# HGRN2 in a two-layer streaming encoder: all products inside the chunks of a group issued in one step, the levels prepared one group ahead

## The chip, the cores and the metric

The kernel runs on one core of a Trainium2 chip. The metric is the device time of one execution in microseconds; of the kernel before there are three runs.

## What is computed

Each of two layers is `x <- x + W_out . concat[mLSTM | retention | SSD | HGRN2](RMSNorm(x) W_in)` for 1024 tokens of a new stream and 8 running streams of 16 tokens. The change lies in HGRN2, a recurrence with a forget decay of each channel, computed here in chunks:

```python
def hgrn_block(s_prev, xs):
    q, k, v, lf = xs
    b = jnp.cumsum(lf, axis=2)
    diff = b[:, :, :, None, :] - b[:, :, None, :, :]
    w = jnp.exp(jnp.where(causal_tril(l)[:, :, None], diff, -jnp.inf))
    s = jnp.einsum("bhtk,bhsk,bhtsk->bhts", q, k, w)
    o = jnp.einsum("bhts,bhsv->bhtv", s, v) + jnp.einsum("bhtk,bhkv->bhtv", q * jnp.exp(b), s_prev)
    s_new = jnp.exp(bl)[..., None] * s_prev + jnp.einsum("bhsk,bhsv->bhkv", k * jnp.exp(bl[:, :, None, :] - b), v)
```

The decay is a vector over the channels, so the scores `s` of a chunk aren't one product of queries and keys: each block of the lower triangle needs queries and keys that refer to a token between them.

## The kernel before

The residual stream is feature-major and lies in SBUF in nine chunks of 128 tokens (eight of the prompt, one with the 8 x 16 sample tokens), in three groups of three chunks. Weight slabs of 256 columns stream once per layer. Weights and activations are split into two parts (hi and lo), and three matmuls per k tile add hi x hi, lo x hi and hi x lo: lines 422 to 424 for products with tokens on the partitions, 401 to 403 with features there. A projection k step below is such a triple.

The mixers are units: four of HGRN2 (h0 to h3, one per head), and pairs of heads of mLSTM (m), retention (r) and SSD (s). The order in a layer is h0, r0, s0, m0, h1, r1, s1, m1, h2, h3, then the two halves of the output projection. The mixer of a unit is a generator (`mix`) and runs beside the projection of the next unit: h0 beside r0, h1 beside r1, h2 beside h3, h3 beside the output projection. `merge` interleaves them: it takes a mixer step whenever the share of steps done falls behind the share of projection steps done, times a pace (0.9 for h beside h, whose last 6 steps go on into the next unit; 1 for h beside r). So the number `steps` of a unit sets how far apart its steps lie. `self.after(1, f)` puts f off by one mixer step, `self.later` by projection steps. There is one queue per engine, in the order in which the program issues; TensorE does what stands there in order, so a matmul that waits holds up the projection behind it.

In HGRN2 `ev_qf` (lines 1413 to 1443) makes queries, keys and running sums of decays from the projection's results, and `fours` (1445) refers the decays to the middle of four tokens, with two products on GpSimd. In `mix`, for each group:

- `base` (1536) multiplies keys and queries inside blocks of 32 tokens, 12 matmuls of 32 columns (line 1544), of which the triangles of four tokens are wanted; it also clears two tiles on GpSimd (1546, 1547), and a copy under a mask takes the result one step later (1548).
- `level` (1524) prepares one of five levels, with blocks of 64, 32, 16, 8 and 4 tokens (li = 0 to 4): two subtractions on VectorE, an exponential on ScalarE, and one step later a product with the keys on GpSimd and one with the queries on VectorE (all products and differences go through the helper at line 210).
- `pick` (1553) multiplies one level, 12 matmuls of 16 columns for levels 2 to 4 (line 1562), 3 of 64 x 64 or 6 of 32 x 32 for levels 0 and 1 (1574), and copies the result one step later. `diag` puts the blocks of 32 into the scores' tile ST.
- `prep` decays queries and keys for the state, `keys` transposes the keys (1594), `state` (1613) and `state_s` (1634) update the states, `out` (1652, 1654) forms the outputs, `post` norms and scales them (1672), `fin` transposes them back (1681).

The main loop takes six steps per group: base, then levels 0 to 4, with `level` three levels ahead, and the output of the group before beside them. At the start the first two levels are prepared over five steps (in h0 and h1; three in h2 and h3):

```python
for li in range(-1, NLEV):
    if li < 0:
        base(g, W)
        prep(g, W)
    else:
        pick(g, W, li)
    if li + LOOK < NLEV:
        level(W, g, li + LOOK)
```

Of the kernel before, what the change touches and what calls it, by code (L numbers as in the profile page):

```python
# [26 lines left out]
D = 1024  # L27
# [16 lines left out]
# the order of the mixers (their projections; a mixer works beside the next one's projection), and the  # L44
# feature tiles of the mixed sequence that each half of the output projection takes
# [73 lines left out]
class Kernel:  # L119
# [24 lines left out]
    # ---- tiles  # L144
# [25 lines left out]
    # ---- work put off by a number of projection steps, so that the tensor engine doesn't wait for it  # L170
# [13 lines left out]
    # ---- the same by a number of mixer steps: what waits for another engine is issued when that is done  # L184
# [11 lines left out]
    # ---- small helpers  # L196
# [21 lines left out]
    # ---- setup  # L218
# [24 lines left out]
    def vectors(self):  # L243
        """Per-channel vectors, brought to channel-on-partition form by one transpose each."""
# [61 lines left out]
    # ---- weight slabs  # L306
# [129 lines left out]
    # ---- residual, norms  # L436
# [4 lines left out]
    def fetch_x(self, g):  # L441
        """Token-major input halves [chunk][half] of group g."""
# [93 lines left out]
    # ---- gates  # L536
# [8 lines left out]
    # ---- per-layer gate preparation  # L545
    def gate_prep(self, l, gt):
# [9 lines left out]
        # SSD: softplus, decays  # L556
# [4 lines left out]
        self.sg = sg  # dt, b, exp(b), exp(total - b), exp(total), exp(total) of the sample streams  # L561
# [47 lines left out]
        # mLSTM: input gates, stabilisers  # L609
# [91 lines left out]
    def streams_in(self, po, zq, state, first):  # L701
        """Adds what the states before the streams give to the sample chunk, in column tiles of two streams."""
# [4 lines left out]
    def km(self, src, which):  # L707
        """For each stream src [128 tokens, 128] with the other streams' rows set to zero."""
# [11 lines left out]
    # ---- mLSTM  # L720
# [247 lines left out]
    # ---- retention  # L968
# [167 lines left out]
    # ---- SSD  # L1136
# [270 lines left out]
    # ---- HGRN2  # L1407
    def unit_h(self, l, h):
# [76 lines left out]
        def mix():  # L1485
# [29 lines left out]
            def prep(g, W):  # L1515
                # decayed queries and keys for the state
# [19 lines left out]
            def base(g, W):  # L1536
                """Groups of four tokens; like the levels inside 32 tokens, in column tiles of 32 tokens, the result by
                token of the tile."""
                sc = self.ps("sc")
                for c in range(3):  # L1540
                    for j in range(4):
                        rs = slice(32 * j, 32 * j + 32)
                        ts = slice(128 * c + 32 * j, 128 * c + 32 * j + 32)
                        nc.tensor.matmul(sc[rs, 32 * c:32 * c + 32], k[g][:, ts], q[g][:, ts], start=True, stop=True)
# [3 lines left out]
                self.after(1, lambda: nc.vector.copy_predicated(D, self.lev[:, LEVW - 96:], sc[:, 0:96]))  # L1548

            def pick(g, W, li):  # L1550
                hs = 64 >> li
# [459 lines left out]
```

## Time and profile before

| | us |
|---|---|
| runs, median of 3 | 2415.31 |
| runs, lowest and highest | 2415.06, 2416.91 |
| span of the profiled execution | 2412.0 |
| TensorE busy in it | 2341.9 (97%) |
| VectorE busy | 1382.3 (57%) |
| ScalarE busy | 1078.9 (45%) |
| GpSimd busy | 933.7 (39%) |
| mean granted clock of TensorE | 0.993 |

The profile gives one execution. Its span runs from the first to the last instruction; the time of a run is taken around it. Matmuls are pipelined: their records overlap, and what one costs is read from start to start. A matmul of fp32 operands leaves two records, so 12 matmuls of the fours are 24 in the timeline. A busy share is an average over stages with different limits, so it doesn't tell what a change in one stage is worth.

### The profile page before, as it was taken

The numbers are of one execution on the slowest core, as the hardware profiler recorded it, in microseconds if no ns is written. First come the engines' busy times: TensorE is split into PE (matmuls) and PEld (weight loads), VectorE is DVE, ScalarE is ACT, GpSimd is POOL, SyncE is SP. The second block draws the span as 40 slices with busy tenths as digits, with TensorE's granted clock in tenths as the row PEclk, the third lists the DMA queues.
The fourth block names the chain that finished last, engine by engine and source line by source line (L and its number), as shares of the span: only waits on it lengthen the run. The fifth ranks groups of instructions, "written<-read, shape, count | busy, mean of one in ns | idle before, by whom it ended". The sixth has DMA issues, their size and how long they took to land.

```text
span 2412.0 us, 50123 instructions
## 1 busy us (share of the span) xinstructions
PE 2341.9 (97%) x19264; PEld 2239.2 (93%) x19264; DVE 1382.3 (57%) x3491; ACT 1078.9 (45%) x2780; POOL 933.7 (39%) x1107
## 2 busy tenths in 40 slices
PE   7999999999999999999989999999999999899998
PEld 7899999999999988899988999999899999889998
DVE  4756753673765366544367376536737654666443
ACT  6344573434555345433244445634344653454332
POOL 2442344253334235423136333432633452345353
PEclk9999999999999999999999999999999999999999
DMA  5112233221123222536411212322111333125552
GB/s 151 37 49 57 71 89 77 67 59 52 49 83 95 71 62 74 158 116 212 133 37 38 61 54 83 86 69 72 48 50 53 100 75 82 49 84 168 161 168 82
DMA packets 273738, 204.09 MB, mean 85 GB/s; under 512 B 57908, under 2 KB 264140, under 8 KB 273500
## 3 DMA queue, kind: packets, MB, share of 16 engines
q1 hardware_dynamic: 273180, 200.81, 29.1%
q8 instruction: 152, 2.49, 0.5%
q14 instruction: 86, 0.70, 0.1%
q0 software_dynamic: 320, 0.09, 0.0%
HBM read 148.53 MB, written 52.29 MB: 83 GB/s over the span
## 4 chain that ended last, share of the span: by engine, by line
PE 86%; DVE 7%; ACT 3%; issue 2%; DMA 1%; POOL 1%; SPq 0%; DVEq 0%; ACTq 0%; POOLq 0%
PE w L422 12%; PE w L401 12%; PE w L424 11%; PE w L423 11%; PE w L402 11%; PE w L403 11%; DVE f L210 3%; ACT f L213 2%; PE w L1299 1%; PE w L1652 1%; PE w L1562 1%; PE w L1613 1%; DVE c L210 1%; PE w L486 1%; PE w L1052 1%
## 5 line engine op out<-in xcount | busy, mean ns | idle before, releaser
L422 PE MATMUL w<-hi,hnh 128*128 128x256 f32 (+1 forms) x2592 | 767.4, 296 | 0.0
L424 PE MATMUL w<-hi,hnl 128*128 128x256 f32 (+1 forms) x2592 | 730.7, 282 | 1.6 <-DVE hnl L489 1.4
L423 PE MATMUL w<-lo,hnh 128*128 128x256 f32 (+1 forms) x2592 | 729.8, 282 | 0.0
L422 PEld LDWEIGHTS w<-hi,hnh 128*128 128x128 f32 x2592 | 492.7, 190 | 11.4 <-issue 7.7
L424 PEld LDWEIGHTS w<-hi,hnl 128*128 128x128 f32 x2592 | 490.9, 189 | 2.2 <-DVE hnl L489 2.0
L423 PEld LDWEIGHTS w<-lo,hnh 128*128 128x128 f32 x2592 | 491.6, 190 | 1.2
L213 ACT ACTIVATE f<-f 128x384 f32<-128x384 f32 (+1 forms) x475 | 244.1, 516 | 435.1 <-DVE f L210 271.9
L213 ACT ACTIVATE c<-c 128x512 f32<-128x512 f32 (+3 forms) x398 | 211.8, 534 | 286.3 <-DVE c L543 205.4
L210 POOL TENSOR_TENSOR f<-f,f 128x384 f32<-128x384 f32 (+2 forms) x268 | 226.6, 853 | 286.3 <-ACT f L213 211.8
L401 PE MATMUL w<-hnh,hi 128*128 128x384 f32 x960 | 336.1, 350 | 0.0
L210 POOL TENSOR_TENSOR lo<-raw,hi 128x512 fp32r<-128x512 f32 x148 | 195.3, 1320 | 346.1 <-ACT hi L200 293.6
L403 PE MATMUL w<-hnh,lo 128*128 128x384 f32 x960 | 324.8, 338 | 0.0
L402 PE MATMUL w<-hnl,hi 128*128 128x384 f32 x960 | 324.3, 338 | 0.0
L401 PE MATMUL w<-mxh,hi 128*128 128x384 f32 x768 | 267.4, 348 | 0.0
L403 PE MATMUL w<-mxh,lo 128*128 128x384 f32 x768 | 259.7, 338 | 0.0
L402 PE MATMUL w<-mxl,hi 128*128 128x384 f32 x768 | 259.5, 338 | 0.0
L210 POOL TENSOR_TENSOR c<-c,c 128x512 f32<-128x512 f32 (+2 forms) x120 | 129.7, 1089 | 229.5 <-ACT c L213 187.0
L210 DVE TENSOR_TENSOR lo<-raw,hi 128x512 fp32r<-128x512 f32 x140 | 112.8, 806 | 135.8 <-ACT hi L200 135.6
L401 PEld LDWEIGHTS w<-hnh,hi 128*128 128x128 f32 x960 | 181.7, 189 | 6.8 <-issue 5.9
L402 PEld LDWEIGHTS w<-hnl,hi 128*128 128x128 f32 x960 | 181.6, 189 | 0.0
L403 PEld LDWEIGHTS w<-hnh,lo 128*128 128x128 f32 x960 | 181.1, 189 | 0.0
L210 DVE TENSOR_TENSOR c<-c,w 128x384 f32<-128x384 f32 (+1 forms) x124 | 73.4, 595 | 184.9 <-PE w L403 116.9
(302 smaller groups left out, 3892.8 us busy)
## 6 DMA issues: line engine op xcount, KB each, us to landing
raw<-in_w_in SPq DMA_DIRECT2D x224, 128.0 KB
raw<-in_w_in SPq DMA_DIRECT2D x112, 256.0 KB
c<-mixd SPq DMA_DIRECT2D x96, 192.0 KB
raw<-in_w_out SPq DMA_DIRECT2D x64, 256.0 KB
xd<-c SPq DMA_DIRECT2D x66, 192.0 KB
mixd<-c SPq DMA_DIRECT2D x48, 256.0 KB
c<-xd SPq DMA_DIRECT2D x60, 192.0 KB
c<-sscr SPq DMA_DIRECT2D x36, 256.0 KB
```

Of the source, the lines that this page charges most:

```text
L210: (self.nc.vector if e == "v" else self.nc.gpsimd).tensor_tensor(out=out, in0=a, in1=b, op=op)
L213: self.nc.scalar.activation(out=out, in_=in_, func=func, scale=scale, bias=bias, **k)
L401: nc.tensor.matmul(o, hi[:, k, ms], xhi[:, k, :], start=(k == 0), stop=False)
L402: nc.tensor.matmul(o, hi[:, k, ms], xlo[:, k, :], start=False, stop=False)
L403: nc.tensor.matmul(o, lo[:, k, ms], xhi[:, k, :], start=False, stop=(k == KT - 1))
L422: nc.tensor.matmul(o, xhi[:, k, ts], hi[:, k, :w], start=(k == 0), stop=False)
L423: nc.tensor.matmul(o, xhi[:, k, ts], lo[:, k, :w], start=False, stop=False)
L424: nc.tensor.matmul(o, xlo[:, k, ts], hi[:, k, :w], start=False, stop=(k == KT - 1))
L486: nc.tensor.matmul(ps[:, cs], tiles[cc][k // 4][:, 128 * (k % 4):128 * (k % 4) + 128], dg[:, cs], start=True, stop=True)
L1052: nc.tensor.matmul(po[h], w[:, h], v[j][:, i, h], start=(c in (0, 8)), stop=(c == 0 or (c < 8 and h == 1)))
L1299: nc.tensor.matmul(po[:, 64 * h:64 * h + 64], pt[:, h], x_[:, 64 * h:64 * h + 64], start=True, stop=True)
L1562: nc.tensor.matmul(sc[rs, 16 * c:16 * c + 16].rearrange("p (n t) -> p n t", t=hs), xt, half(xt), start=True, stop=True)
```

## The change

The instructions are the same on every engine, apart from their order. `base` and `pick` become `fresh` (the two clears) and `gram`, which issues the products of the fours and all five levels at once into two PSUM tiles; one step later a single function makes all the copies out of them. A group takes five steps instead of six: `gram` with the first output chunk of the group before; `keys` with the other two; `post`; `state`; `fin`. The levels of the next group are prepared in its first three steps, two, two and one, with `prep` beside the last and `fresh` a step later. For the first group these are four steps ahead of the first `gram`, without the empty steps of before. `steps` is 29 for all units (it was 31 for h0 and h1). Shortened:

```diff
-            def base(g, W):
-                sc = self.ps("sc")
...
-                self.after(1, lambda: nc.vector.copy_predicated(D, self.lev[:, LEVW - 96:], sc[:, 0:96]))
-            def pick(g, W, li):
...
+            def fresh(W):
+                W["ST"], W["D"] = ST, D = self.f(), self.t(96)
+                nc.gpsimd.memset(ST, 0.0)
+                nc.gpsimd.memset(D, 0.0)
+            def gram(g, W):
+                sc, sb = self.ps("sc"), self.ps("sc")
+                half = lambda a, hs: a.rearrange("p (n e t) -> p n e t", e=2, t=hs)[:, :, 1]
+                mm = lambda o, a, b_: nc.tensor.matmul(o, a, b_, start=True, stop=True)
+                at = lambda li: 96 + 48 * (li - 2)
+                for c in range(3):
+                    for j in range(4):
+                        ts = slice(128 * c + 32 * j, 128 * c + 32 * j + 32)
+                        mm(sc[32 * j:32 * j + 32, 32 * c:32 * c + 32], k[g][:, ts], q[g][:, ts])
+                for li in range(2, NLEV):
...
+                            mm(o.rearrange("p (n t) -> p n t", t=hs), xt, half(xt, hs))
+                for li in (1, 0):
...
+                            mm(sb[64 * j:64 * j + hs, 192 * li + hs * c:192 * li + hs * c + hs], xt[:, 0:hs], xt[:, hs:2 * hs])
+                def evac():
...
+                    diag(W)
+                self.after(1, evac)
...
-            for _ in range(2 if h < 2 else 0):
-                yield
             level(Ws[0], 0, 0)
-            yield
             level(Ws[0], 0, 1)
-            for _ in range(2 if h < 2 else 2):
-                yield
+            yield
+            level(Ws[0], 0, 2)
+            level(Ws[0], 0, 3)
+            yield
+            level(Ws[0], 0, 4)
+            fresh(Ws[0])
+            yield
+            prep(0, Ws[0])
+            yield
             for g in range(NG):
                 W = Ws[g]
...
+                V = Ws[g - 1] if g > 0 else None
+                for s in range(5):
+                    if s == 0:
+                        gram(g, W)
+                        if V:
+                            out(g - 1, V, 0)
+                    elif s == 1:
                         keys(g, W)
...
+                    if g + 1 < NG:
+                        for li in ((0, 1), (2, 3), (4,), (), ())[s]:
+                            level(Ws[g + 1], g + 1, li)
+                        if s == 2:
+                            prep(g + 1, Ws[g + 1])
+                        if s == 3:
+                            fresh(Ws[g + 1])
                     yield
...
-        return dict(runs=[("tm", ev_vg), ("fm", ev_qf)], mix=mix, steps=31 if h < 2 else 29, ...
+        return dict(runs=[("tm", ev_vg), ("fm", ev_qf)], mix=mix, steps=29, ...
```

Where instructions went is seen in three places. On TensorE, at the first group of h1 beside r1, the fours (line 1544) stood alone between projection matmuls, before:

```order
L423 MATMUL w_6227<-lo_5728,hnh_231 128x256
L424 MATMUL w_6227<-hi_5727,hnl_232 128x256
L1544 MATMUL w_6237<-f_5725,f_5787 32x32 x12
L422 MATMUL w_6227<-hi_5727,hnh_231 128x256
L423 MATMUL w_6227<-lo_5728,hnh_231 128x256
L424 MATMUL w_6227<-hi_5727,hnl_232 128x256
```

and now (line 1547 is the one matmul call of `gram`):

```order
L424 MATMUL w_6162<-hi_5703,hnl_232 128x256
L1547 MATMUL w_6219<-f_5701,f_5763 32x32 x12
L1547 MATMUL w_6219<-f_6104 32x16 x12
L1547 MATMUL w_6219<-f_6108 32x16 x12
L1547 MATMUL w_6219<-f_6143 32x16 x12
L1547 MATMUL w_6220<-f_6075 32x32 x6
L1547 MATMUL w_6220<-f_6071 64x64 x3
L422 MATMUL w_6162<-hi_5703,hnh_231 128x256
```

All six products stand together, five k steps of the projection ahead of where the fours stood (923 k steps into the kernel, now 918; in h2 beside h3 1671 and now 1675).

On GpSimd at the same place, from the last decayed queries and keys (two products of 128x384) on; c are tiles of r1's rotary embedding, lo is the weight split. Before:

```order
L210 TENSOR_TENSOR f722_6039<-f722_6039,f729_6082 128x384
L210 TENSOR_TENSOR f726_6068<-f726_6068,f730_6083 128x384
L210 TENSOR_TENSOR lo15_6129<-raw15_0_5731,hi15_6128 128x2x256
L210 TENSOR_TENSOR c735_6154<-c733_6150,c734_6151 128x8x32
L210 TENSOR_TENSOR c735_6154<-c734_6151,c733_6150 128x8x32
L210 TENSOR_TENSOR c735_6154<-c735_6154,cst_107 128x512
L210 TENSOR_TENSOR f732_6140<-f732_6140,f685_5787 128x3x64
L210 TENSOR_TENSOR f737_6176<-f737_6176,f685_5787 128x6x32
```

and now:

```order
L210 TENSOR_TENSOR f708_6015<-f708_6015,f715_6058 128x384
L210 TENSOR_TENSOR f712_6044<-f712_6044,f716_6059 128x384
L210 TENSOR_TENSOR f718_6071<-f718_6071,f671_5763 128x3x64
L210 TENSOR_TENSOR f719_6075<-f719_6075,f671_5763 128x6x32
L210 TENSOR_TENSOR lo15_6125<-raw15_0_5707,hi15_6124 128x2x256
L210 TENSOR_TENSOR f720_6104<-f720_6104,f671_5763 128x12x16
L210 TENSOR_TENSOR f721_6108<-f721_6108,f671_5763 128x24x8
L1538 MEMSET f723_6147 128x384
L1539 MEMSET t724_6148 128x96
L210 TENSOR_TENSOR c727_6158<-c725_6154,c726_6155 128x8x32
L210 TENSOR_TENSOR c727_6158<-c726_6155,c725_6154 128x8x32
L210 TENSOR_TENSOR c727_6158<-c727_6158,cst_107 128x512
```

The next row is level 4, `f722_6143`. Levels 0 to 3 and the clears now stand ahead of the rotary products, and level 4 right behind them.

On VectorE in h2 beside h3, around the scaling of the second group's output (line 1672). Before:

```order
L543 TENSOR_SCALAR f_11839<-w_11786 128x384
L1425 SCALAR_TENSOR_TENSOR f_11841<-f_11841,oml,f_11840 128x384
L1427 TENSOR_SCALAR f_11839<-f_11839 128x384
L1434 SCALAR_TENSOR_TENSOR f_11839<-ones,f_11839 128x128 x3
L210 TENSOR_TENSOR lo_11760<-raw_1_11241,hi_11759 128x2x256
L210 TENSOR_TENSOR t_11859<-f_11839 128x96
L1453 SCALAR_TENSOR_TENSOR f_11860<-t_11859,f_11839 128x384
L1458 TENSOR_SCALAR f_11839<-t_11859 128x384
L1566 COPY_PREDICATED t_11692<-lev,w_11814 128x2x16
L1672 SCALAR_TENSOR_TENSOR f_11824<-w_11742,s_11823,c_10333 128x128
L1672 SCALAR_TENSOR_TENSOR f_11824<-w_11742,s_11823,c_10462 128x128 x2
```

and now (the line is 1678):

```order
L1678 SCALAR_TENSOR_TENSOR f_11749<-w_11678,s_11748,c_10285 128x128
L1678 SCALAR_TENSOR_TENSOR f_11749<-w_11678,s_11748,c_10414 128x128 x2
L1629 SCALAR_TENSOR_TENSOR f_11781<-f_11571,bl_11038,w_11778 128x128
L1629 SCALAR_TENSOR_TENSOR f_11781<-f_11781,bl_11038,w_11778 128x128
L543 TENSOR_SCALAR f_11815<-w_11782 128x384
L1425 SCALAR_TENSOR_TENSOR f_11817<-f_11817,oml,f_11816 128x384
L1427 TENSOR_SCALAR f_11815<-f_11815 128x384
L1434 SCALAR_TENSOR_TENSOR f_11815<-ones,f_11815 128x128 x3
```

The scaling now stands ahead of the gate chain of h3's projection (lines 543 to 1458) instead of behind it.

## Rows read from the trace of the kernel before

**Rows 1.** The page's head and totals: busy us, share of the span, instructions, by engine.

```profile
span 2412.0 us, 50123 instructions
...
PE 2341.9 (97%) x19264; PEld 2239.2 (93%) x19264; DVE 1382.3 (57%) x3491; ACT 1078.9 (45%) x2780; POOL 933.7 (39%) x1107
```

**Rows 2.** Waits of TensorE by line and releaser: us in total, times, longest.

```profile
PE w L1594 <- DVE f L210: 12.2, 8, 2.9
...
PE w L1681 <- DVE f L1672: 8.1, 3, 3.1
...
PE w L1574 <- POOL f L210: 6.9, 4, 3.2
PE w L1562 <- POOL f L210: 4.6, 6, 1.2
PE w L1613 <- ACT f L200: 4.4, 7, 0.7
```

**Rows 3.** TensorE's timeline, h1 beside r1: start us, us, line, operation, records.

```profile
502.94 0.28 PE L424 MATMUL w<-hi,hnl 128*128 128x256 f32 x1
503.14 0.40 PE L1544 MATMUL w<-f,f 128*32 128x32 f32 x24
503.47 0.39 PE L422 MATMUL w<-hi,hnh 128*128 128x256 f32 x1
...
505.93 0.28 PE L424 MATMUL w<-hi,hnl 128*128 128x256 f32 x1
506.14 0.56 PE L1574 MATMUL w<-f 128*64 128x64 f32 x6
506.63 0.38 PE L422 MATMUL w<-hi,hnh 128*128 128x256 f32 x1
506.85 0.28 PE L423 MATMUL w<-lo,hnh 128*128 128x256 f32 x1
```

**Rows 4.** TensorE's timeline, level 3 and the state product, second group.

```profile
538.21 0.38 PE L1562 MATMUL w<-f 128*32 128x16 f32 x24
538.52 0.94 PE L1613 MATMUL w<-c,f 128*128 128x128 f32 x6
```

**Rows 5.** GpSimd's timeline, h1 beside r1, in brackets the idle time before.

```profile
497.22 2.14 POOL L210 TENSOR_TENSOR f<-f,f 128x384 f32<-128x384 f32 x2 [1.73 <-ACT f L213]
499.32 1.41 POOL L210 TENSOR_TENSOR lo<-raw,hi 128x512 fp32r<-128x512 f32 x1
500.69 1.54 POOL L210 TENSOR_TENSOR c<-c,c 128x256 f32<-128x256 f32 x2
502.31 1.40 POOL L210 TENSOR_TENSOR c<-c,cst 128x512 f32<-128x512 f32 x1
503.67 1.27 POOL L210 TENSOR_TENSOR f<-f,f 128x192 f32<-128x192 f32 x2
...
508.05 0.41 POOL L1546 MEMSET f<- 128x384 f32 x1
```

**Rows 6.** VectorE's timeline, h1 beside r1.

```profile
496.41 0.62 DVE L210 TENSOR_TENSOR f<-f 128x192 f32<-128x192 f32 x2
...
498.41 2.53 DVE L210 TENSOR_TENSOR f<-f 128x192 f32<-128x192 f32 x2
```

**Rows 7.** VectorE and TensorE where h0 beside r0 starts; TensorE where h2 beside h3 does.

```profile
97.45 0.59 DVE L210 TENSOR_TENSOR f<-f 128x192 f32<-128x192 f32 x2
...
99.68 0.40 PE L1544 MATMUL w<-f,f 128*32 128x32 f32 x24
...
896.70 0.40 PE L1544 MATMUL w<-f,f 128*32 128x32 f32 x24
```

**Rows 8.** Stretches: their length, busy us of five engines, granted clock, DMA share, GB/s.

```profile
907.40:910.80 3.40, 3.17 (x37) 2.84 (x37) 2.57 (x5) 0.79 (x2) 3.07 (x4) 0.50 0.04 13
...
917.40:934.70 17.30, 15.88 (x221) 14.48 (x220) 13.42 (x37) 8.81 (x27) 7.19 (x11) 1.00 0.21 63
523.50:544.90 21.40, 21.40 (x272) 20.37 (x272) 17.51 (x48) 10.16 (x28) 13.22 (x21) 1.00 0.26 73
```

More of the change, by code (lines that the diff above doesn't have):

```diff
@@ L1558, in pick @@
                     for c in range(n):
                         for j in range(4):
-                            rs = slice(32 * j, 32 * j + 32)
                             xt = x[:, 128 * c + 32 * j:128 * c + 32 * j + 32]
-                            nc.tensor.matmul(sc[rs, 16 * c:16 * c + 16].rearrange("p (n t) -> p n t", t=hs), xt, half(xt),
-                                             start=True, stop=True)
-                    cp = lambda a: a.rearrange("p (n t) -> p n t", t=hs)
-                    mk = self.lev[:, 48 * (li - 2):48 * (li - 2) + 16 * n]
@@ L1566, in pick @@
-                    self.after(1, lambda: nc.vector.copy_predicated(half(D[:, 0:32 * n]), cp(mk), cp(sc[:, 0:16 * n])))
-                    if li == NLEV - 1:
-                        self.after(1, lambda: diag(W))
-                    return
-                for c in range(n):
-                    for j in range(64 // hs):
-                        rs = slice(64 * j, 64 * j + hs)
-                        xt = x[:, 128 * c + 64 * j:128 * c + 64 * j + 2 * hs]
-                        nc.tensor.matmul(sc[rs, hs * c:hs * c + hs], xt[:, 0:hs], xt[:, hs:2 * hs], start=True, stop=True)
@@ L1576, in put @@
-                def put():
-                    for j in range(64 // hs):
-                        rs = slice(64 * j, 64 * j + hs)
-                        self.copy(sv(W["ST"][rs], n)[:, :, 64 * j + hs:64 * j + 2 * hs],
-                                  sc[rs, 0:hs * n].rearrange("p (c t) -> p c t", t=hs), BIG[li])
-                self.after(1, put)
+                            o = sc[32 * j:32 * j + 32, at(li) + 16 * c:at(li) + 16 * c + 16]
+                            mm(o.rearrange("p (n t) -> p n t", t=hs), xt, half(xt, hs))
@@ new lines, in gram @@
+                for li in (1, 0):
+                    hs = 64 >> li
+                    x, w = W["X"].pop(li)
+                    widths[li] = n = w // 128
+                    for c in range(n):
+                        for j in range(64 // hs):
+                            xt = x[:, 128 * c + 64 * j:128 * c + 64 * j + 2 * hs]
+                            mm(sb[64 * j:64 * j + hs, 192 * li + hs * c:192 * li + hs * c + hs], xt[:, 0:hs], xt[:, hs:2 * hs])
+                def evac():
+                    D = W["D"]
+                    nc.vector.copy_predicated(D, self.lev[:, LEVW - 96:], sc[:, 0:96])
+                    for li in range(2, NLEV):
+                        hs, n = 64 >> li, widths[li]
+                        cp = lambda a: a.rearrange("p (n t) -> p n t", t=hs)
+                        mk = self.lev[:, 48 * (li - 2):48 * (li - 2) + 16 * n]
+                        nc.vector.copy_predicated(half(D[:, 0:32 * n], hs), cp(mk), cp(sc[:, at(li):at(li) + 16 * n]))
+                    for li in (0, 1):
+                        hs, n = 64 >> li, widths[li]
+                        for j in range(64 // hs):
+                            rs = slice(64 * j, 64 * j + hs)
+                            self.copy(sv(W["ST"][rs], n)[:, :, 64 * j + hs:64 * j + 2 * hs],
+                                      sb[rs, 192 * li:192 * li + hs * n].rearrange("p (c t) -> p c t", t=hs), BIG[li])
+                    diag(W)
@@ L1691, in mix @@
             SS = {}
-            for _ in range(2 if h < 2 else 0):
-                yield
             level(Ws[0], 0, 0)
+            level(Ws[0], 0, 1)
             yield
-            level(Ws[0], 0, 1)
-            for _ in range(2 if h < 2 else 2):
-                yield
+            level(Ws[0], 0, 2)
[6 more added lines that the diff above has]
+            yield
             for g in range(NG):
                 W = Ws[g]
-                for li in range(-1, NLEV):
-                    if li < 0:
-                        base(g, W)
-                        prep(g, W)
-                    else:
-                        pick(g, W, li)
-                    if li + LOOK < NLEV:
-                        level(W, g, li + LOOK)
-                    elif g + 1 < NG:
-                        level(Ws[g + 1], g + 1, li + LOOK - NLEV)
-                    if li == 1:
-                        keys(g, W)
-                    if li == 3:
+                V = Ws[g - 1] if g > 0 else None
[5 more added lines that the diff above has]
+                    elif s == 1:
+                        keys(g, W)
+                        if V:
+                            out(g - 1, V, 1)
+                            out(g - 1, V, 2)
+                    elif s == 2 and V:
+                        post(g - 1, V)
+                    elif s == 3:
                         state(g, W)
@@ L1716, in mix @@
                             load_states()
-                    if g > 0:
-                        V = Ws[g - 1]
-                        for cc in {0: (0,), 1: (1, 2)}.get(li, ()):
-                            out(g - 1, V, cc)
-                        if li == 2:
-                            post(g - 1, V)
-                        if li == 4:
-                            fin(g - 1, V)
-                            Ws[g - 1] = None
+                    elif s == 4 and V:
+                        fin(g - 1, V)
+                        Ws[g - 1] = None
+                    if g + 1 < NG:
[5 more added lines that the diff above has]
+                            fresh(Ws[g + 1])
                     yield
@@ L1742, in mix @@
             yield
-        return dict(runs=[("tm", ev_vg), ("fm", ev_qf)], mix=mix, steps=31 if h < 2 else 29, gate=(lambda: self.gate_prep(l, gt)) if h == 0 else None)
+        return dict(runs=[("tm", ev_vg), ("fm", ev_qf)], mix=mix, steps=29, gate=(lambda: self.gate_prep(l, gt)) if h == 0 else None)
     def mix_load(self, l, half, g):
```

16 lines of the change are left out of this document (4 added, 12 removed).

## The prediction

> **What bounds the kernel now.** I read the totals of the page first, then the waits of TensorE, then the timelines of the places where the change acts. TensorE is busy 97% of a span of 2412.0 us [rows 1]; VectorE (57%) and GpSimd (39%) have room on average. So time can only come from what TensorE does between the projection's matmuls, from its waits, or from its clock. The waits at HGRN2's lines sum to 12.2 + 8.1 + 6.9 + 4.6 + 4.4 = 36.2 us [rows 2]; they sit at the first group of a unit and in the stretch of h2 beside h3. The runs' median is 2415.3 us, 3.3 above the profiled span; I take what lies around the span as unchanged, make the sum on the span and add it to the median. A difference under 0.2% (4.8 us) can't be told from none.
>
> **Part 1, fewer bursts on TensorE.** A burst of small products inside the projection costs more than its own matmuls. For level 0 alone the last projection matmul starts at 505.93 and the second one after the burst at 506.85: 0.92 us where two ordinary pitches take 0.235 (0.117 each), a price of 0.68 [rows 3]. For the fours the step back begins 0.53 after the last projection matmul; with the same slow first pitch behind it (0.22) and less 0.235 that is 0.51. Level 2 stands alone like the fours: 0.50. Level 3 has the state product behind it: 0.31 from its start to that product, 0.21 to get in as with the fours, less the 0.12 that would pass without it: 0.40 [rows 4]; levels 1 and 4 (ahead of the key transposes and of the last transposes) cost 0.40 each by the same pattern. A group pays 0.51 + 0.68 + 0.50 + 3 x 0.40 = 2.9 us. The one burst that replaces them issues the same matmuls. Inside the fours' burst 503.47 - 503.14 = 0.33, less one pitch to get out, for 24 records: 0.0087 each. So 96 records of fours and levels 2 to 4 take 0.83; level 1 about 0.18 and level 0 about 0.36 (0.49 less 0.13); getting in 0.08, out 0.13, the slow first pitch 0.10: 1.7 us. That is **1.2 us a group**, 24 groups (8 units of 3): **-28.8 us**. The copies that follow are the same instructions one step later; their result is wanted by the group's output products five steps on, so they cost nothing; were VectorE a whole group behind, those products would wait.
>
> **Part 2, the waits of before.** All 36.2 us go: levels are no longer taken one at a time, and the 8.1 us on the scaling (three times, where it stood in VectorE's queue behind a whole gate chain) go because the scaling is moved ahead of that chain. **-36.2 us.** What is late next is part 3.
>
> **Part 3, the first group of a unit.** Before, TensorE took the fours first and a level every step behind them. Now all six have to be there at once, at a place five projection k steps (5 x 0.354 us, three matmuls of 0.118) before that of the fours in h0 and h1, and four k steps behind it in h2 beside h3. I walk h1 beside r1. The burst is due at 503.1 - 1.8 = 501.3 [rows 3]. The decayed queries and keys leave GpSimd at 497.22 + 2.14 = 499.4 [rows 5]. From there its new order is levels 0 and 1 (0.64 each, half of 1.27), the weight split lo (1.41), levels 2 and 3 (1.27), two clears (0.41 and, a quarter as wide, an estimated 0.1), three rotary products of r1 (1.54 + 1.40), level 4 (0.64): 8.0 us without one wait, so 507.4 at the earliest. It will wait: two subtractions of VectorE that feed it took 0.62 us while GpSimd was idle and 2.53 us beside GpSimd's products [rows 6]; they get through as the GpSimd instruction ends. Letting each VectorE operation with two such inputs end after the GpSimd one that it meets, lo starts at 503.1 (its hi comes behind four exponentials), levels 2 and 3 are done at 505.8, the clears at 506.4, the rotary products at 509.1, level 4 at 509.7: a wait of **8.3 us**. The bounds are 6.1 (nothing waits) and 10.5 (2.2 more, as far on the other side). I take 8.3, since rows 6 show that they wait.
> [...]
> The same walk for h0 beside r0: VectorE starts the first subtraction at 97.45, behind the gate preparation; TensorE is due at 99.7 - 1.8 = 97.9 [rows 7]. In h1 level 4 ended 13.3 us after that subtraction began, with the decayed queries and keys in front on GpSimd; here these are over, 1.9 us less: 108.9, a wait of **11.0**. For h2 beside h3: due at 896.7 + 1.4 = 898.1 [rows 7]; there are no rotary products, but lo stands ahead of level 4 and its hi behind five exponentials: by the walk the fifth ends at 905.1, and hi, lo (1.41) and level 4 (0.64) bring it to 907.5, a wait of **9.4**. All three occur in both layers: **+57.4 us**. h3's burst beside the output projection comes so late (its steps are spread over a slower projection) that I see no wait there.
>
> **Part 4, later groups.** In h1 beside r1 VectorE was busy 17.5 of 21.4 us of a group [rows 8]; a group now has 37 k steps instead of 42 and cheaper bursts, 13.1 + 4.4 = 17.5 us, and some 16.7 of VectorE's work (17.5 less an estimated 0.8 for the copies of five k steps): 0.5 us of wait each, eight groups, +4. In h2 beside h3 it was 13.4 of 17.3 [rows 8]. Of these 28 k steps are 9.9; the other 7.4 hold bursts and some 1.8 of waits; without the waits, with 1.2 less of bursts and with 24 k steps a group has 12.9: it comes to VectorE's own pace and waits some 1.5, four groups, +6. Together **+10.0 us** (0 if VectorE's work fits; 4.4 a group in h2 if it keeps its 17.3 us).
>
> **Part 5, the clock.** [...] Five waits at HGRN2's bursts had such a stretch: -8.5. Six long waits take their place, 1.7 each: **+1.7 us**. The bound on the other side is a stretch twice as long at each, +10 more.
> [...]
>
> **Sum:** -28.8 - 36.2 + 57.4 + 10.0 + 1.7 = +4.1, so 2415.3 + 4.1 = **2419.4 us: no change that can be told**, by a little. What the fewer bursts and the old waits give, the wait at the first groups takes.
>
> **Rivals.** (a) *Faster: the levels are ready sooner.* With the six first waits at their lower bounds (2.2 less each, -13.2) and VectorE keeping up in the later groups (-10), the time is 2396; with half of both 2408. For: the bound of 507.4 is a plain sum of rows, and while TensorE stands VectorE gets no new projection results to copy. Against: rows 6. (b) *Slower: VectorE becomes the bound behind the first group.* Groups in h2 that keep their 17.3 us wait 4.4 each, four of them 11.6 more than in the sum; with 0.5 more at the other eight it is 2435, at half of that 2427. It decides at once, from 0.1 us a group more than in the sum. For: 16.7 against 17.5 and 13.4 against 12.9. Against: part of that busy time is time blocked by GpSimd. (c) *The burst is no burst*: if TensorE paid the way in and out between its parts, the saving of part 1 would be gone: 2448. Against: the fours run over three column offsets and four tiles without such a gap.
>
> **Chances.** Forecast 0.38 (0.28 within 0.2% of before, 0.10 above), (a) 0.30, all faster, (b) 0.28 and (c) 0.04, slower. Faster by over 0.2%: 0.30; within: 0.28; slower: 0.42. The range from 2398 to 2436 leaves out the far ends of (a) and (b) and all of (c); the forecast's own is 2411 to 2425.
>
> **What would show it.** Right: TensorE's waits in HGRN2 become six long ones at the new burst's line, of 8 to 11 us, released by GpSimd, each with a stretch at half clock; a burst of 1.7 us where nothing waits; no wait on the scaling. Wrong: first waits of 5 us or less (then a), waits of over 3 us in the second and third group of h2 (then b), a gap between the burst's parts (then c), or any wait in h3.

## The result, and the profile after

The changed kernel takes 2436.92 us (median of 4 runs, 2436.11 to 2438.9) against 2416.11 of before (2415.06 to 2416.96): a ratio of 1.0086, 95% interval 1.0071 to 1.0101. It is 20.8 us slower. Forecast was no change (2419, range 2398 to 2436). Single executions that took over 4% longer than the others of their kernel are left out of the times and ratios below.

The head of the page and its totals after, beside [rows 1]:

```profile
span 2435.1 us, 49910 instructions
...
PE 2326.2 (96%) x19264; PEld 2244.9 (92%) x19264; DVE 1354.7 (56%) x3443; ACT 1073.3 (44%) x2764; POOL 916.1 (38%) x1091
```

TensorE is busy 16 us less in a span that is 23 us longer. The totals show also that the change is not one of order alone: VectorE has 48 instructions fewer, ScalarE and GpSimd 16 each. The loop before also prepared levels of the next group,

```python
if li + LOOK < NLEV:
    level(W, g, li + LOOK)
elif g + 1 < NG:
    level(Ws[g + 1], g + 1, li + LOOK - NLEV)
```

so that at `li = 4` it made level 2 of the next group, and made it again at that group's `li = -1`. The change makes it once: 16 preparations fewer (second and third groups of 8 units), each of three instructions on VectorE and one on ScalarE and GpSimd. GpSimd's products with the keys fall from 104 to 96 in the shape 128x192, that of the second groups, and from 32 to 24 in 128x128, that of the third.

The waits of TensorE by line and releaser after (in total, times, longest), beside [rows 2]; line 1547 is the burst, 1860 the flip of the residual in the output projection, 1687 the transposes back (the last ones here), 1619 the state product, 507 the sums of squares for a layer's norm:

```profile
PE w L1547 <- POOL f L210: 56.5, 20, 5.9
PE w L1860 <- DMA c<-in_x_prompt: 10.3, 3, 5.1
PE w L507 <- DVE f L210: 8.8, 2, 5.4
...
PE w L1687 <- DVE f L1678: 8.7, 1, 8.7
PE w L1619 <- ACT f L200: 3.7, 5, 1.3
```

and the two of these lines that the kernel before had at 1848 and 507:

```profile
PE w L507 <- DVE f L210: 7.6, 2, 4.2
...
PE w L1848 <- DMA c<-in_x_prompt: 4.2, 2, 3.5
```

All 36.2 us of [rows 2] are gone, and 56.5 + 8.7 + 3.7 = 68.9 stand in their place, with 7.3 more at lines 1860 and 507. Both kernels issue the same 12,960 projection matmuls in one order, so the start of the same one can be compared. Units by their projection, with the delay that each adds to the same matmul:

| stretch | added us, first layer | second layer |
|---|---|---|
| h0 beside r0 | +4.8 | +3.9 |
| h1 beside r1 | +4.2 | +2.7 |
| h2 beside h3 | -2.0 | -3.7 |
| h3 beside the output projection | +2.9 | +9.9 |
| the end of the layer's output projection | +0.9 | 0.0 |

In h2 the change gains, and what follows loses more than that.

The first burst of h1 beside r1, on TensorE; in brackets what it waited for:

```profile
505.98 0.40 PE L1547 MATMUL w<-f,f 128*32 128x32 f32 x24
509.69 0.38 PE L1547 MATMUL w<-f 128*32 128x16 f32 x24 [3.31 <-POOL f L210]
510.55 0.38 PE L1547 MATMUL w<-f 128*32 128x16 f32 x24 [0.48 <-POOL f L210]
514.82 1.70 PE L1547 MATMUL w<-f 128*32 128x16 f32 x42 [3.88 <-POOL f L210]
```

and GpSimd over the same time, beside [rows 5]:

```profile
501.83 3.65 POOL L210 TENSOR_TENSOR f<-f,f 128x384 f32<-128x384 f32 x4 [1.73 <-ACT f L213]
507.39 1.46 POOL L210 TENSOR_TENSOR lo<-raw,hi 128x512 fp32r<-128x512 f32 x1 [1.91 <-ACT hi L200]
508.82 1.68 POOL L210 TENSOR_TENSOR f<-f,f 128x192 f32<-128x192 f32 x2
510.44 0.42 POOL L1538 MEMSET f<- 128x384 f32 x1
510.79 0.18 POOL L1539 MEMSET t<- 128x96 f32 x1
510.94 1.85 POOL L210 TENSOR_TENSOR c<-c,c 128x256 f32<-128x256 f32 x2
512.86 1.24 POOL L210 TENSOR_TENSOR c<-c,cst 128x512 f32<-128x512 f32 x1
514.06 1.78 POOL L210 TENSOR_TENSOR f<-f,f 128x192 f32<-128x192 f32 x2
```

This is the walk of the prediction: lo waits 1.9 us for its hi, then levels 2 and 3 (508.82), the clears, the rotary products, and level 4 as the first of the two products at 514.06, and TensorE's last 42 records start as it ends. From 507.39 to 514.06 GpSimd has no gap of over 0.1 us, so level 4's product stood in its queue. The three waits sum to 7.7 us (8.3 predicted). The six first bursts of h0, h1 and h2 wait 7.8, 7.7 and 7.8 us in the first layer and 9.3, 8.7 and 9.1 in the second, 50.2 in all. Where nothing waits, in h3 beside the first layer's output projection, the burst is what part 1 said, 1.7 us from 1018.63 to the return at 1020.33:

```profile
1018.36 0.33 PE L403 MATMUL w<-mxh,lo 128*128 128x384 f32 x1
1018.63 0.40 PE L1547 MATMUL w<-f,f 128*32 128x32 f32 x24
1018.84 1.56 PE L1547 MATMUL w<-f 128*32 128x16 f32 x90
1020.33 0.44 PE L401 MATMUL w<-mxh,hi 128*128 128x384 f32 x1
```

The last transposes of h2 in the second layer wait for the scaling (line 1678), which stands on VectorE behind the end of h3's last gate chain (1458):

```profile
2199.35 1.24 DVE L1453 SCALAR_TENSOR_TENSOR f<-t,f 128x384 f32<-128x384 f32 x1
2200.69 0.36 DVE L1458 TENSOR_SCALAR f<-t 128x384 f32<-128x384 f32 x1
2200.97 0.86 DVE L1678 SCALAR_TENSOR_TENSOR f<-w,s,c 128x128 f32<-128x128 f32 x3
```

```profile
2201.37 0.99 PE L1687 MATMUL w<-cst,f 128*128 128x128 f32 x3 [8.69 <-DVE f L1678]
```

Stretches of half clock after, beside [rows 8] (length, busy us of TensorE, its weight loads, VectorE, ScalarE, GpSimd, then the granted clock):

```profile
101.90:112.14 10.24, 6.21 (x106) 5.82 (x107) 6.93 (x10) 2.70 (x6) 6.50 (x10) 0.50 0.20 54
511.50:518.33 6.83, 3.51 (x51) 3.33 (x52) 5.02 (x7) 1.57 (x3) 4.26 (x5) 0.50 0.14 38
910.90:921.14 10.24, 5.96 (x105) 5.56 (x106) 6.83 (x20) 5.78 (x15) 7.37 (x10) 0.50 0.10 31
...
2197.70:2204.53 6.83, 3.16 (x11) 3.02 (x12) 3.99 (x10) 4.48 (x11) 4.36 (x6) 0.50 0.01 2
```

Not 3.4 us each at the six first bursts but 6.8 to 10.2. Inside the span the stretches at 0.50 sum to 97.5 us, with TensorE busy in 59.1 of them; before these were 33.4 and 29.1. Half of the 30.0 more is 15 us, an estimate that takes work at 0.50 to last twice as long; in the stretch at 511.50 projection matmuls of 256 columns start 0.213 us apart, behind it 0.118, 1.8 times, which would make it some 13.

**The sum again, with what was measured.** Bursts -28.8 (as predicted), old waits -36.2, burst +56.5, last transposes +8.7, state +3.7, lines 1860 and 507 +7.3, clock +15.0: +26.2, where the span grew by 23.1. The first term is not measured by itself, but TensorE's busy time holds it together with the clock's: it fell by 15.7, so with +15.0 of clock the bursts gave some 30.7, and the sum is 24.3. Other small waits are some 1 us shorter.

### The profile page after: what moved, and what is told of

It is laid out like the page before. It is cut to its first block, busy times and chain, and to the rows that moved or that the text cites. A ratio compares the mean times of both kernels' runs of the same rounds, so it can differ in the third digit from the quotient of the medians.

```text
span 2435.1 us, 49910 instructions
## 1 busy us (share of the span) xinstructions
PE 2326.2 (96%) x19264; PEld 2244.9 (92%) x19264; DVE 1354.7 (56%) x3443; ACT 1073.3 (44%) x2764; POOL 916.1 (38%) x1091
## 4 chain that ended last, share of the span: by engine, by line
PE 82%; DVE 7%; ACT 4%; issue 2%; POOL 2%; DMA 2%; SPq 0%; DVEq 0%; ACTq 0%; POOLq 0%
PE w L422 11%; PE w L401 11%; PE w L424 11%; PE w L423 11%; PE w L403 11%; PE w L402 11%; ACT f L213 3%; DVE f L210 2%; PE w L1547 1%; PE w L1299 1%; POOL f L210 1%; POOL c L210 1%; PE w L486 1%; PE w L1052 1%; PE w L819 1%
## 5 line engine op out<-in xcount | busy, mean ns | idle before, releaser
L213 ACT ACTIVATE f<-f 128x384 f32<-128x384 f32 (+1 forms) x459 | 232.7, 517 | 334.5 <-DVE f L210 162.7
L210 POOL TENSOR_TENSOR f<-f,f 128x384 f32<-128x384 f32 (+2 forms) x252 | 215.6, 871 | 241.4 <-ACT f L213 159.0
L210 DVE TENSOR_TENSOR lo<-raw,hi 128x512 fp32r<-128x512 f32 x140 | 118.3, 845 | 166.5 <-ACT hi L200 166.3
```

Source lines behind the costliest of these rows:

```text
L210: (self.nc.vector if e == "v" else self.nc.gpsimd).tensor_tensor(out=out, in0=a, in1=b, op=op)
L213: self.nc.scalar.activation(out=out, in_=in_, func=func, scale=scale, bias=bias, **k)
```

## The experiments

Theory F: the loss is the wait at the six first bursts and the half clock behind them. Theory T: it is lost in the tail of h2 and in h3 beside the output projection. The times below are medians with the ratio to before from the same session; line numbers are those of each kernel, so the burst is 1547 and the flip 1860 or 1862.

| kernel | us | ratio to before, 95% interval |
|---|---|---|
| the change | 2436.92 | 1.0086 (1.0071 to 1.0101) |
| e1_late | 2421.35 | 1.0015 (1.0006 to 1.0025) |
| e2_first_old | 2427.52 | 1.0042 (1.0025 to 1.0059) |
| e4_two | 2426.07 | 1.0040 (1.0027 to 1.0053) |
| e5_warm, again | 2429.82, 2432.04 | 1.0059 (1.0039 to 1.0078), 1.0073 (1.0051 to 1.0095) |
| e8_carry | 2441.33 | 1.0102 (1.0079 to 1.0125) |
| e11_prefetch | 2439.01 | 1.0090 (1.0067 to 1.0112) |
| e10_dve | 2426.08 | 1.0045 (1.0029 to 1.0062) |
| e9_two_late_carry | 2434.36 | 1.0074 (1.0055 to 1.0094) |
| e13_two_late_state | 2414.48 | 0.9992 (0.9983 to 1.0002) |
| e13_state_dve | 2409.45 | 0.9976 (0.9964 to 0.9987) |
| e14_before_dve | 2416.10 | 1.0000 (0.9990 to 1.0009) |
| e17_keys | 2407.41 | 0.9967 (0.9956 to 0.9978) |
| e3_tail | 2428.27 | 1.0052 (1.0038 to 1.0066) |
| e18_keys_tail | 2403.36 | 0.9948 (0.9935 to 0.9962) |

**More time ahead of the first burst.**

```diff
             prep(0, Ws[0])
             yield
+            yield
+            yield
             for g in range(NG):
...
-        return dict(..., mix=mix, steps=29, ...
+        return dict(..., mix=mix, steps=31, ...
```

> The change with two more empty mixer steps ahead of the first burst of a unit (steps 31 instead of 29). Theory F (the loss is the wait at the six first bursts, 59 us in the profile of the change, and the half clock behind them): each wait falls by two mixer steps, about 5 us in h0 and h1 and 3.3 in h2, some 26 us in all, and the clock comes back sooner: 2404 to 2412 us. Theory V (VectorE and GpSimd are the bound and the wait only moves): the later bursts wait instead, 2430 or more.

2421.35: between the two. The waits of TensorE in it:

```profile
PE w L1547 <- POOL f L210: 30.0, 15, 3.8
PE w L1619 <- ACT f L200: 13.0, 6, 2.8
```

The waits at the burst fell by 26.5 us, just the 26 that F gave, but the state product waits 9.3 more, and the busy time at half clock stayed (60.4 us; the granted clock was 0.983 in the profiled run, 0.980 in that of the change). F is right about where the wait is; two of its consequences were wrong: that nothing waits next, and that a wait of 4 us saves the clock that one of 9 loses.

**The first group as before** (`base` and `pick` for the first group in six steps, the levels of the second group in the third to fifth of them, `gram` for the other two groups; 31 steps in h0 and h1).

> The first group of each unit as before (fours and levels one per step, three levels ahead), groups two and three as in the change. Theory F: the six first waits go back to the some 28 us that the first groups waited before, with half the stretches of half clock, the saving of 1.2 us on 8 first groups is lost: 2400 to 2408 us. Theory T (the loss lies in the tail of h2 and in h3 beside the output projection): it stays, 2425 or more.

2427.52, in T's range, but not for T's reason: 9.4 us of the loss came back, against some 29 to 37 by F. The burst of the second group waits instead (14.7 us at the burst's line), with 10.0 + 7.0 + 5.6 us in the first group and 7.6 at the last transposes: 44.9 us, more than the 36.2 of before. So the first group's burst isn't all of the loss: the second group's, whose levels were prepared in three steps, waits too when the first group keeps the old order.

**Level 4 ahead of the rotary products.**

```diff
             level(Ws[0], 0, 1)
-            yield
             level(Ws[0], 0, 2)
+            yield
             level(Ws[0], 0, 3)
-            yield
             level(Ws[0], 0, 4)
+            yield
             fresh(Ws[0])
```

> The change with the first group's levels in two steps, three and two, and the clears a step later, so that level 4's product on GpSimd stands ahead of the two clears and, in h0 and h1, of the rotary products. Theory Q (GpSimd's queue sets the last level): the first bursts of h0 and h1 wait some 3 us less each, 2422 to 2428 us. Theory L (VectorE, held up by GpSimd's products, sets it): within 3 us of the change, 2434 to 2440.

2426.07, as theory Q had it: -10.9 us from an order of a few instructions. The burst waits 36.1 us instead of 56.5, of which 14.9 are now released by VectorE; the state product 7.6 more. The edit also starts level 4's subtractions and exponential a step sooner, so it doesn't try GpSimd's queue by itself.

**Work in the gap, to price the clock.**

```diff
                 at = lambda li: 96 + 48 * (li - 2)
+                if g == 0 and h < 3:
+                    for _ in range(10):
+                        mm(sc[:, 0:G3], k[g][:, 0:128], k[g])
                 for c in range(3):
```

> The change with ten matmuls of 384 columns more ahead of the first burst in h0, h1 and h2, whose results are overwritten: some 6.6 us of work inside a wait of 9. The records show 32 us of TensorE work at half clock behind the six first bursts of the change. Theory C (the clock falls because TensorE stands still): these stretches go, some 16 us: 2419 to 2424 us. If the clock falls for another reason, or the added work doesn't fit the wait: 2437 or more.

> The same kernel as e5_warm, for its profile: the profiled execution of that one took 8019 us. The time of its other runs was some 4 us below that of the change, not the 16 expected. Either the stretches of half clock stay (the added matmuls don't keep the clock), or they go and TensorE waits longer elsewhere. 2429 to 2436 us; with the clock kept, the sum of half-clock stretches falls from 100 to under 60 us.

2429.82 and 2432.04 (ratios 1.0059 and 1.0073, the change 1.0086): 3 to 7 us faster than the change, not 16. Single runs lie between 2429.0 and 2435.5; the profiled one took 2429.08, 8.1 us less than that of the change. The added matmuls ahead of the burst of h1 beside r1 (first row) and the stretch that was at half clock in the change:

```profile
504.52 6.29 PE L1547 MATMUL w<-f 128*128 128x384 f32 x19
```

```profile
511.50:518.33 6.83, 5.29 (x90) 5.09 (x79) 6.18 (x16) 2.05 (x5) 4.39 (x6) 1.00 0.16 41
```

Here the clock holds at 1.00. Inside the span the half-clock stretches sum to 56.9 us, 41.1 of them busy: 18.0 less busy time at half clock than in the change, worth some 9 by the estimate above (8 at the pitches given there), of which the profiled run shows 8.1. Of the six stretches at first bursts the two of h1 are gone; the other four are left at 3.4, 3.4, 3.4 and 6.8 us (107.1, 922.9, 1305.2 and 2114.1) for 10.2 each, and there 2.1 to 3.4 us of wait were left too (1.5 and 2.8 in h1). So with work in the wait the clock held at 1.00 (two bursts) or the stretch at 0.50 was shorter (four): at these bursts it fell because TensorE stood still. The first expectation had this cause, but its 16 us only in part; the second had the time and the sum.

**The tail, by the scaling and by the loads.** `CARRY = dict(hh=4)` instead of 6; and the first residual tiles fetched at `n == 7` instead of 9.

> The change with 4 instead of 6 steps of h2's mixer left to the output projection, so that the last group's scaling stands on VectorE ahead of h3's last gate chain and not behind it. In the profile of the change TensorE waits 8.7 us for that scaling in the second layer and 6.3 us at the first burst of h3 behind it. Theory S (the place of the scaling makes both waits): both go, 2422 to 2429 us. Theory K (the stretch from h3's gates to the output projection is a chain of fixed length through gates, weight splits and loads; TensorE, which comes early to it, waits at another place instead): within 3 us of the change, 2434 to 2440.

> The change with the first two residual tiles of the output projection fetched two half accumulation groups earlier. In the first layer the change waits 10.3 us for these loads where the kernel before waits 4.2. Theory D (the place of these loads on SP's queue makes the wait): some 6 us go, 2429 to 2433 us. Theory K (SP's queue is held up by loads that wait for weight splits behind h3's gate chain): within 3 us of the change, 2434 to 2440.

2439.01 is in K's range; 2441.33 is 1.3 above it, and far from S's. Neither is faster than the change. With the scaling ahead of the gate chain its wait is gone, and three others have come:

```profile
PE w L1547 <- POOL f L210: 64.2, 22, 9.9
...
PE w L402 <- POOL mxl L210: 2.4, 2, 1.8
PE w L401 <- ACT mxh L200: 2.4, 1, 2.4
```

The longest, 9.9 us, is h3's first burst in the second layer, where the waits of the change sum to 5.0; lines 401 and 402 wait for the split of the output projection's inputs. With the earlier loads the flip waits 12.6 us instead of 10.3.

**Key products on VectorE.**

```diff
-                    self.tt(xv(X)[:, :, 0], xv(X)[:, :, 0], xv(k[g])[:, :, 0], ALU.mult, "p")
+                    self.tt(xv(X)[:, :, 0], xv(X)[:, :, 0], xv(k[g])[:, :, 0], ALU.mult)
```

> The change with the key products of all levels on VectorE instead of GpSimd. Theory Q (GpSimd's queue sets the last level at the first bursts): five products leave that queue, the first bursts of h0 and h1 wait some 3 us less each and those of h2 about 1.5 less: 2420 to 2428 us. Theory V (VectorE is the bound): it has five products of 0.35 us more per group, the later bursts wait longer: 2440 or more.

2426.08, as theory Q had it. VectorE, which has 120 products more (5 levels, 24 groups), isn't the bound: the burst waits 20.1 us less, all of it now on VectorE, the state 7.1 more.

```profile
PE w L1547 <- DVE f L210: 36.4, 20, 5.6
PE w L1619 <- ACT f L200: 10.8, 8, 2.5
```

As a control, the same edit on the kernel before:

> The kernel before with the key products of the levels on VectorE. If GpSimd's products hold up the preparation in every order, this is faster too: of its waits those released by GpSimd (11.5 us) go, 2405 to 2411 us. If only the bunched order of the change makes them matter: within 4 us of before.

2416.10, no change. The waits released by GpSimd are gone, but VectorE now releases 4.5 us at line 1574 and the key transposes (line 1594) wait 4.1 more: 34.9 us in all for 36.2. So the place of these products is worth 11 us where five levels are wanted at once, and nothing where they are taken one by one.

**Three cures together.** e1_late, e4_two and e8_carry:

> The change with three things together: two more empty steps ahead of the first burst (steps 31), the first group's levels in two steps, and 4 steps of h2 left to the output projection. If the first bursts are what costs and both cures add, the first bursts wait under 2 us each: 2403 to 2411 us, faster than the kernel before. If the stretch of h3 beside the output projection keeps its some 12 us: 2413 to 2420.

2434.36: neither. The waits and, below, the place of the longest (ScalarE's timeline, then TensorE's, first group of h0 beside r0):

```profile
PE w L1619 <- ACT f L200: 39.1, 9, 6.3
...
PE w L1547 <- POOL f L210: 8.2, 10, 2.1
PE w L1547 <- DVE f L210: 5.0, 2, 3.1
```

```profile
119.35 0.52 ACT L213 ACTIVATE f<-f 128x384 f32<-128x384 f32 x1 [4.18 <-DVE f L210]
120.61 0.52 ACT L213 ACTIVATE f<-f 128x384 f32<-128x384 f32 x1 [0.74 <-DVE f L210]
121.16 0.49 ACT L200 ACTIVATE f<-w 128x384 f32<-128x384 f32 x1
```

```profile
121.70 1.65 PE L1619 MATMUL w<-c,f 128*128 128x128 f32 x6 [5.96 <-ACT f L200]
```

The bursts wait 13 us in all, and the state product takes over: it needs the copy of the transposed keys (121.16), and that stands on ScalarE behind two exponentials of the next group's levels, which wait for VectorE. So at this place the levels that are prepared a group ahead stand in the way of the group that is due.

**The state a step later, and the keys a step earlier.** e1_late and e4_two with `state` moved from the fourth step to the fifth; then also with e10_dve; then also with `keys` in the first step, behind the burst (the diff shows this one, shortened, without the edits of e1_late, e4_two and e10_dve).

```diff
                     if s == 0:
                         gram(g, W)
                         if V:
                             out(g - 1, V, 0)
+                        keys(g, W)
                     elif s == 1:
-                        keys(g, W)
...
-                    elif s == 3:
-                        state(g, W)
-                        if g == 1:
-                            load_states()
-                    elif s == 4 and V:
-                        fin(g - 1, V)
...
+                    elif s == 3 and g == 1:
+                        load_states()
+                    elif s == 4:
+                        state(g, W)
+                        if V:
+                            fin(g - 1, V)
...
```

> The change with two more empty steps ahead of the first burst, the first group's levels in two steps, and the state product one step later (with the last transposes). With the first two of these the first bursts waited 13 us in all, but the state products 39 us, for a copy of ScalarE that stands behind the next group's exponentials. Theory O (that order on ScalarE makes the state's wait): the wait goes, and with it most of what the first bursts cost: 2403 to 2411 us, faster than before. Theory V (the preparation of a group takes its time on VectorE and GpSimd whatever the order): TensorE waits at the second bursts or the state instead, 2418 to 2430.

> The same with the key products of the levels on VectorE instead of GpSimd, which alone gave 11 us. Theory O: 2400 to 2408 us. Theory V (VectorE is the bound): VectorE has 1.8 us more per group, so slower than the kernel without this, 2420 to 2435. If what GpSimd does to VectorE's two-input operations is the bound: faster than it by 5 to 10 us.

> The fastest kernel so far (two more empty steps, the first group's levels in two steps, state one step later, key products on VectorE), with the key transposes right behind the burst, a step earlier, so that the copy of the transposed keys stands on ScalarE ahead of two of the next group's exponentials. TensorE waits 22 us there for that copy. Theory O (order on ScalarE): most of that goes, 2393 to 2402 us. Theory V (VectorE's pace is reached): the second bursts wait instead, 2406 to 2412.

2414.48, 2409.45 and 2407.41. The first is level with before, 22 us below the change and 3.5 above theory O's range: the state product still waits 17.1 us. The second is 5.0 us below the first, 1.5 above O's range, where VectorE as the bound would have made it slower; in it the state product waits 22.0. In the third that is gone, but the keys' transposes of the first groups wait for VectorE's decayed keys and the transposes back for the scaling:

```profile
PE w L1687 <- DVE f L1678: 14.8, 5, 9.0
PE w L1600 <- DVE f L210: 13.3, 7, 3.8
```

Of the 22 us the medians show 2.0. The time is theory V's, the place isn't: the second bursts wait under 1 us each. Order and spacing alone, with no work moved between engines (the first), were worth 22 us against the change. In it the bursts and the state product wait 29.6 us instead of 60.2, and yet TensorE is busy at half clock for 79.5 us, more than in the change (59.1); the granted clock was 0.980 in the profiled run of each.

**The last transposes later.** Two steps more ahead of the last `fin`, in the change and in e17_keys.

> The change with two more empty steps ahead of the last transposes of a unit. In the second layer these wait 8.7 us for the scaling, which stands behind h3's last gate chain; two steps later they'd wait some 4. Theory S: 2429 to 2434 us. Theory K (a chain of fixed length through gates, weight splits and loads to the output projection): h3's first burst or the output projection wait instead, 2434 to 2440.

> e17_keys and e3_tail together: the time of e17_keys less 3 to 6 us by theory S, within 2 us of it by theory K.

2428.27 and 2403.36: -8.7 and -4.1, theory S, though its range for the first began at 2429. In e3_tail:

```profile
PE w L401 <- ACT mxh L200: 2.6, 1, 2.6
...
PE w L402 <- POOL mxl L210: 2.5, 3, 1.5
```

The change's wait of 8.7 us on the scaling is gone and h3's first burst behind it no longer waits (5.0 us in the change), against 5.1 of new waits at lines 401 and 402: 8.6 in all. K falls for the second layer: moving the scaling (e8_carry) only brought the next wait forward, moving its user gave TensorE projection work to do meanwhile. In the first layer the wait at the flip, 9.1 to 12.6 us in every kernel in which the burst replaces the old products, was touched by neither; its cause stays open. **e18_keys_tail is faster than both kernels**, 0.9948 (0.9935 to 0.9962) of before. How much of that the burst gives and how much the 16 preparations that are no longer made twice isn't shown: the kernel before without them wasn't run.

## Why the prediction was wrong

**Part 1 was right.** The burst takes 1.7 us where nothing waits, and busy time and clock together give some 30.7 us for the 28.8.

**Part 2 was half right.** The levels' single waits went. That the wait on the scaling goes failed: at the groups in the middle of h2 the scaling does stand ahead of the gate chain, but the last group's scaling, which the order rows didn't show, is still behind h3's last one, and the user of it, the last transposes, came eleven projection k steps earlier (3953 k steps into the kernel, 3964 before): one wait of 8.7 us for three of 8.1 in all. e3_tail shows it.

**Part 3 was right for the six first bursts in place and releaser, and somewhat high in size**: 50.2 us for 57.4, furthest off in h0 (7.8 and 9.3 for 11.0). With h3's 5.0 in the second layer, where no wait was expected and which comes behind the same late tail, and 1.3 at the second bursts of h2, this is the 56.5 at line 1547. The walk's bound through GpSimd's queue is seen in GpSimd's rows above; e4_two and e10_dve, 11 us each, agree with it, though each moves something else too. That VectorE's subtractions are held up by GpSimd's products [rows 6], on which the walk leaned, the trace of the kernel before shows well beyond those rows: 103 subtractions of 128x192 that met no GpSimd product took 0.32 to 0.35 us, 105 that met one 0.34 to 1.46, 0.80 in the mean; the two of [rows 6] that start at 498.41 and 499.50 ended at 499.57 and 500.94, each 0.21 us behind the end of the GpSimd product beside it. What it cost at the bursts wasn't tried by itself: e10_dve takes products off the queue as well as out of VectorE's way.

**Part 4 was too high, and looked at the wrong place**: the later bursts waited little (0.6 us at each second burst of h2, nothing in h0 and h1), while 3.7 us came at the state product and 6.1 at the flip, neither of which had a term. It also counted on the same work on VectorE but for the copies; each second and third group has one preparation of a level less.

**Part 5 failed most.** "Six long waits take their place, 1.7 each" was taken from one place [rows 8] with shorter waits (2.0 and 2.9 us). No run shows the 1.7 itself: it is half of the 3.4 us at 0.50 there, an estimate; in that stretch projection matmuls of 256 columns start 0.213 us apart, behind it 0.118. At waits of 7.7 to 9.3 us the clock stayed at 0.50 for 6.8 to 10.2 us, 32.5 us of them busy at the six. +1.7 was predicted, some +15 is the estimate from the records (13 at the pitches measured). e5_warm_again shows the cause at these bursts (work in the wait, and 1.00 at two of the six, 0.50 for 3.4 to 6.8 us at four), and 8.1 us of the price in its profiled run. What sets the length of a stretch stays open: e1_late cut the waits at the bursts from 56.5 to 30.0 us and left the busy time at half clock where it was.

Terms missed: clock 13.3, last transposes 8.7, flip and line 507 7.3, state 3.7, less 10.9 at the bursts (67.4 predicted with part 4, 56.5 measured): 22.1, and 4.1 + 22.1 = 26.2 is the sum above. That the measured time lies within 1 us of the end of the range is luck: bursts put too high stood against four terms put too low or left out. Rival (b) had the sign and, at 2435, nearly the time, but another mechanism: the second bursts of h2 waited 0.6 us each, released by GpSimd, where (b) had 4.4 for VectorE.

## What to carry to other kernels

Putting several small products into one burst saves the way in and out of each (some 30.7 us here), but makes the burst wait for the last of its operands (56.5 us here): count, queue by queue, what stands ahead of that operand, and begin its preparation before you merge. Work that is prepared a step ahead stands in the queues in front of what is due now (39.1 us of waits at the state product in e9_two_late_carry); where a wait is cured, look at the next consumer on the same queues, since most cures here brought the next wait forward. A wait of TensorE can cost more than its length: in the change the clock was 0.50 for 6.8 to 10.2 us at each of the six long ones. Shorter waits in place of long ones didn't give the clock back (busy at half clock 60.4 us in e1_late and 79.5 in e13_two_late_state, for 59.1; granted clock 0.983 and 0.980, for 0.980), so price it from records like those you expect. And count the instructions of both kernels before you call a change one of order alone.

## What was not expected of the hardware

In the change, at one wait in two pieces (h0 beside r0; 4.1 and 3.6 us, ending at 102.2 and 107.0, with 1.2 of work between), the granted clock was 0.50 for 10.2 us from 101.9, 6.2 of them busy. In the kernel before it was 0.50 for 3.4 us behind waits of 2.9, 2.2, 3.2 and 3.1 us (ending at 906.4, 953.8, 2097.7 and 2151.7), and stayed at 1.00 behind others of 2.4, 2.4 and 2.8 (109.5, 1300.8 and 2188.8). The same two waits of h1, 1.0 and 0.7 us, left it at 1.00 in the first layer (517.3 and 518.4, some 7 us behind one of 0.6) and were followed by 3.4 us of 0.50 in the second (1710.8 and 1711.9, 7 us behind one of 1.9). Ten matmuls in the gap held it at 1.00 at h1 beside r1 in both layers and didn't at four other bursts.
